# RMSNorm with swish on one core: all loads and stores on SyncE's queue in one order, with a ring of 100 rows

## The chip, the cores and the metric

The kernel runs on 1 core of one Trainium2 chip. The metric is the device time of one execution in microseconds (us). The kernel before takes 160.34 us, the median of 3 runs (160.22 to 160.51).

## The reference

The input `x` has 16 x 1024 rows of 512 float32 values; the output has the same shape. Each row is divided by its root mean square, multiplied by `gamma`, and then by its own sigmoid.

```
rms = sqrt(mean(x ** 2, axis=-1) + eps)
x_norm = x / rms * gamma
out = x_norm * (1 / (1 + exp(-x_norm)))        # float32
```

That is 16384 rows of 2 KB: 33.55 MB are read from HBM and 33.55 MB are written.

## The kernel before

The 16384 rows are spread over the 128 partitions, so that each partition holds 128 rows in the course of the run ("rows" below are always these 128 per partition; one such row is 256 KB over all partitions). The list `groups` (L28) says which rows are neighbours in HBM: within a group of n rows each partition's n rows are contiguous, so a transfer of a whole group moves one contiguous piece for each partition.

The rows live in a ring `xb` of 96 slots in SBUF (L29, L71). Row a uses slot a modulo 96, and everything is done in place: the load writes the slot, VectorE normalises it, ScalarE applies the swish, the store reads it. Rows 96 to 127 go into the slots of rows 0 to 31, so their loads have to wait for the stores of these rows.

The work is done in 32 chunks of 4 rows (`cn`, K = 32). For a chunk k:

- ScalarE squares it. Two of its rows are squared one by one with an accumulated sum (L181); the other two go to PSUM in one instruction (L188), and VectorE sums them (`sums`, L234).
- GpSimd adds eps and raises to the power -0.5 (L162, L169).
- VectorE multiplies each row by the scale and by gamma (`norm`, L245).
- ScalarE applies the swish to all four rows in one instruction (L200).

The order on ScalarE is written out by a loop (L223 to L230): the squares of chunk k, then those stores that are due, then the swish of chunk k - 2. VectorE does the sums of chunk k and then the norm of chunk k - 1. The first chunk that touches a newly loaded piece waits for that whole piece to land (L178).

Two queues carry the transfers. All ten loads (`load`, L118) are issued by SyncE in the order of the list `loads`; the first two stand ahead of the start barrier (`early`). Before a load that overwrites slots, SyncE waits until the stores of these slots have landed (L123); the table `behind` adds such a wait for load (96,16), which also waits for store (16,12). The eight stores (`store`, L206) are issued by ScalarE (L210) between its chunks. Each waits for the swish of its last chunk, and the table `hold` keeps the first three until load (64,28) has landed and store (64,32) until load (112,12) has landed. A piece (a, n) is the n rows from row a on. In the end SyncE waits for all stores (L267).

Of the kernel before, what the change touches and what calls it, by code (L numbers as in the profile page):

```python
# [9 lines left out]
def kernel(  # L10
# [7 lines left out]
    nc = tc.nc  # L18
# [5 lines left out]
    xf = x.flatten_outer_dims()  # L24
    of = out.flatten_outer_dims()
    R, D = xf.shape

    groups = [16, 16, 32, 32, 16, 16]  # L28
    ring = 96  # L29
    loads = [(0, 4), (4, 4), (8, 8), (16, 16), (32, 32), (64, 28)]  # L30
    loads += [(92, 4), (96, 16), (112, 12), (124, 4)]
    stores = [(0, 16), (16, 12), (28, 4), (32, 32), (64, 32)]
    stores += [(96, 16), (112, 8), (120, 8)]
    hold = {0: ((64, 28), 12), 3: ((112, 12), 22)}
    behind = {(96, 16): (16, 12)}
    early = 2
    cn = 4
    n_sq = 2
# [9 lines left out]
        assert sum(n for _, n in pieces) == rows_each  # L48

    K = rows_each // cn  # L50
    hold = {t: (loads.index(piece), k) for t, (piece, k) in hold.items()}
    behind = {loads.index(a): stores.index(b) for a, b in behind.items()}
    landings, seen = [], 0
    for k in range(K):
        landings.append([])
# [4 lines left out]
    ends = [-(-(a + n) // cn) for a, n in stores]  # L60
# [20 lines left out]
    ld = [nc.alloc_semaphore(f"ld{t}") for t in range(len(loads))]  # L81
    st = [nc.alloc_semaphore(f"st{t}") for t in range(len(stores))]
# [14 lines left out]
    s_swish = nc.alloc_semaphore("s_swish")  # L97

    def need(ins, sem, value):
        return ins.wait_op(sem, value, "sem-ge")  # L100

    def dram(ap, piece):
        a, n = piece
        g = max(g for g in range(len(groups)) if first[g] <= a)
        r = a - first[g]
        assert r + n <= groups[g], piece
        rows = ap[P * first[g] : P * (first[g] + groups[g])]
        return rows.rearrange("(p n) d -> p n d", n=groups[g])[:, r : r + n, :]

    def buf(piece):  # L110
        a, n = piece
        at = a % ring
        assert at + n <= ring, piece
        return xb[:, at : at + n, :]

    stored_by_sync = set()

    def load(i):  # L118
        a, n = loads[i]
        for u, (c, m) in enumerate(stores):  # L120
            over = c + ring < a + n and a < c + m + ring
            if (over or behind.get(i) == u) and u not in stored_by_sync:
                nc.sync.wait_ge(st[u], 16)  # L123
                stored_by_sync.add(u)
        return nc.sync.dma_start(  # L125
            out=buf(loads[i]), in_=dram(xf, loads[i])
        ).then_inc(ld[i], 16)

    entry = nc.main_func.blocks[0].instructions
    here = nc.cur_bb.bb.instructions  # L130
# [11 lines left out]
    for t in range(early):  # L142
        ins = load(t).ins
        assert here[-1] is ins or here[-1].name == ins.name
        here.pop()
        at = next(
            i for i, other in enumerate(entry)
            if other.engine == mybir.EngineType.SP
            and isinstance(other, mybir.InstDrain)
        )  # L150
        entry.insert(at, ins)
    for t in range(early, len(loads)):
        load(t)
    nc.sync.wait_ge(s_scratch, 16)

    nc.gpsimd.memset(blank, 0.0).then_inc(s_blank, 1)  # L156
# [3 lines left out]
    for k in range(K):  # L160
        need(
            nc.gpsimd.tensor_scalar(  # L162
                out=aeps[:, k, :], in0=ms[:, k, :], scalar1=eps_f, scalar2=None,
# [6 lines left out]
                out=rstd[:, k, :], in0=aeps[:, k, :], in1=neg_half, op=ALU.pow  # L170
# [4 lines left out]
    def square(k):  # L175
        at = k * cn % ring
        for landing in landings[k]:
            nc.scalar.wait_ge(ld[landing], 16)  # L178
        for j in range(n_sq, cn):
            n = k * (cn - n_sq) + j - n_sq  # L180
            acc = nc.scalar.activation(  # L181
                out=junk[n % 2], in_=xb[:, at + j, :], func=AF.Square,
                scale=inv_d**0.5, accum_out=ms[:, k, j : j + 1],
            )
            if n >= 2:
                need(acc, s_acc, n - 1)
            acc.then_inc(s_acc, 1)
        square = nc.scalar.activation(  # L188
            out=sq[k % 2], in_=xb[:, at : at + n_sq, :],
            func=AF.Square, scale=inv_d**0.5,  # L190
        )
        if k >= 2:
            need(square, s_sum, k - 1)
        square.then_inc(s_sq, 1)

    def swish(k):
        at = k * cn % ring
        rows = xb[:, at : at + cn, :]
        need(
            nc.scalar.activation(out=rows, in_=rows, func=AF.Silu), s_norm, k + 1  # L200
        ).then_inc(s_swish, 1)

    def after(t):
        return max((k for u, (_, k) in hold.items() if u <= t), default=0)

    def store(t):  # L206
        if t in hold:
            nc.scalar.wait_ge(ld[hold[t][0]], 16)
        need(
            nc.scalar.dma_start(out=dram(of, stores[t]), in_=buf(stores[t])),  # L210
            s_swish, ends[t],
        ).then_inc(st[t], 16)

    need(nc.scalar.dma_start(out=scratch, in_=blank), s_blank, 1).then_inc(
        s_scratch, 16
    )
# [2 lines left out]
        s_zero, 1,  # L219
    ).then_inc(s_gld, 16)  # L220
    nc.scalar.preload_act_table_set("silu_and_others")  # L221
    stored = 0
    for k in range(K + 3):  # L223
        if k < K:
            square(k)
        while stored < len(stores) and max(ends[stored] + 2, after(stored)) <= k:
            store(stored)
            stored += 1
        if 2 <= k < K + 2:
            swish(k - 2)  # L230

    def sums(k):
# [29 lines left out]
        if k >= 1:  # L262
            norm(k - 1)

    for t in range(len(stores)):
        if t not in stored_by_sync:
            nc.sync.wait_ge(st[t], 16)  # L267


# [33 lines left out]
```

## Time and profile before

| what | value |
|---|---|
| runs | 160.22, 160.34, 160.51 us |
| span of the profiled execution, first to last instruction | 159.3 us (159.28) |
| time of the profiled execution beside its span | not recorded apart; the median of the runs is 1.06 us above the span |
| ScalarE busy | 129.7 us |
| VectorE busy | 124.4 us |
| GpSimd busy | 65.4 us |
| bytes read and written, mean rate over the span | 33.56 MB and 33.56 MB, 421 GB/s |

The issues and landings of the transfers, from the trace (us from the start of the span; "landed" is when the last of the 16 DMA engines that share a transfer has reported):

| transfer | issued | landed |
|---|---|---|
| load (0,4) | 0.00 | 5.55 |
| load (8,8) | 1.90 | 13.04 |
| load (32,32) | 2.77 | 42.10 |
| load (64,28) | 3.27 | 59.04 |
| load (92,4) | 3.83 | 61.51 |
| store (0,16) | 59.11 | 72.06 |
| store (16,12) | 59.49 | 79.13 |
| store (28,4) | 60.60 | 81.53 |
| load (96,16) | 79.22 | 91.31 |
| load (112,12) | 79.58 | 98.58 |
| load (124,4) | 81.54 | 101.06 |
| store (32,32) | 98.66 | 120.41 |
| store (64,32) | 115.86 | 139.78 |
| store (120,8) | 146.47 | 159.23 |

How to read the profile: the page divides the span into 40 equal slices of about 4 us and gives each engine's busy share in tenths. The DMA row is the mean over the core's 16 DMA engines. A packet is counted with its whole duration and size in the slice where it starts, so slices with long packets swing around the mean. Each transfer is shared by the 16 DMA engines, 8 partitions each; each engine works through its own part, so that one transfer has 16 landings, one for each engine.

### The profile page before, as it was taken

To read this page: it belongs to the slowest core of one execution; us is meant where nothing else is said; L and a number is where in the kernel's file an instruction comes from. 1 tells how busy PE (TensorE), PEld (TensorE's weight loads), DVE (VectorE), ACT (ScalarE), POOL (GpSimd) and SP (SyncE) were. 2 spreads that over 40 slices of the span, in tenths; PEclk is the share of its full clock that TensorE was granted. 3 is DMA by queue.
4 is the path that set the end of the run, shared out by engine and by line. 5 is a ranking of instruction groups with operands and counts; after the bars stand their busy time and mean duration, and the time that the engine had idled before them with its cause. 6 is when DMAs were issued, how large, how long until landed. Compare 5 with 4: busy or idle time off the path is not lost.

```text
span 159.3 us, 503 instructions
## 1 busy us (share of the span) xinstructions
DVE 124.4 (78%) x162; ACT 129.7 (81%) x193; POOL 65.4 (41%) x71
## 2 busy tenths in 40 slices
DVE  0049996999289999599999999999999999992000
ACT  0675979997499995999999999999999999945000
POOL 1035553555145555155555555555555555540000
DMA  7999997998999969999899898969969969999997
GB/s 251 448 467 407 411 593 329 510 444 362 461 432 446 461 280 446 477 399 426 370 397 411 387 469 379 609 280 510 527 263 527 527 263 527 395 395 395 440 420 325
DMA packets 2750, 67.17 MB, mean 422 GB/s; under 512 B 437, under 2 KB 437, under 8 KB 441
## 3 DMA queue, kind: packets, MB, share of 16 engines
q1 hardware_dynamic: 1440, 33.56, 49.7%
q10 hardware_dynamic: 1304, 33.57, 49.0%
q14 instruction: 6, 0.04, 0.1%
HBM read 33.56 MB, written 33.56 MB: 421 GB/s over the span
## 4 chain that ended last, share of the span: by engine, by line
ACT 57%; DMA 25%; DVE 4%; issue 3%; ACTq 1%; SPq 0%
ACT xb L200 25%; DMA xb<-in_x_dram 25%; ACT junk L181 18%; ACT sq L188 14%; DVE xb L245 3%; ACTq L210 1%; DVE ms L234 1%; SPq L125 0%; ACTq L178 0%
## 5 line engine op out<-in xcount | busy, mean ns | idle before, releaser
L245 DVE SCALAR_TENSOR_TENSOR xb<-xb,rstd,gamma_sb 128x512 f32<-128x512 f32 x128 | 87.3, 744 | 0.0
L200 ACT ACTIVATE xb<-xb 128x2048 f32<-128x2048 f32 x32 | 60.9, 1903 | 5.0 <-DVE xb L245 3.4
L234 DVE TENSOR_REDUCE ms<-sq 128x2 f32<-128x1024 f32 x32 | 39.2, 1223 | 19.0 <-ACT sq L188 16.0
L162 POOL TENSOR_SCALAR aeps<-ms 128x4 f32<-128x4 f32 x32 | 20.6, 644 | 71.6 <-DVE ms L234 71.6
L169 POOL TENSOR_TENSOR rstd<-aeps,neg_half 128x4 f32<-128x4 f32 x32 | 44.0, 1376 | 2.7
L181 ACT ACTIVATE junk<-xb 128x512 f32<-128x512 f32 x64 | 37.2, 582 | 6.3 <-DMA xb<-in_x_dram 6.3
L188 ACT ACTIVATE sq<-xb 128x1024 f32<-128x1024 f32 x32 | 32.1, 1005 | 0.0
L181 ACT ACTIVATION_READ_ACCUMULATOR junk<-xb 128x1 f32 x64 | 11.9, 186 | 0.0
L221 ACT ACT_TABLE_LOAD x1 | 1.3, 1283 | 5.4 <-issue 5.4
L258 DVE LOAD_MASK_SELECT gamma_sb<-gamma x1 | 0.0, 14 | 1.1 <-DMA gamma<-in_gamma_dram 1.1
L258 DVE STREAM_SHUFFLE gamma_sb<-gamma 128x512 f32<-128x512 f32 x1 | 0.7, 716 | 0.0
L156 POOL MEMSET blank<- 128x16 f32 x1 | 0.1, 111 | 1.1 <-POOLq L66 1.1
L157 POOL MEMSET gamma<- 128x512 f32 x1 | 0.5, 524 | 0.0
L284 POOL MEMSET const-float32-0.0<- 128x1 f32 x1 | 0.1, 98 | 0.7 <-issue 0.7
L284 POOL MEMSET const-bfloat16-1.0<- 128x1 bf16 x1 | 0.1, 101 | 0.0
L284 POOL MEMSET const-uint8-127<- 128x1 uint8 x1 | 0.1, 101 | 0.0
L158 POOL MEMSET neg_half<- 128x4 f32 x1 | 0.1, 101 | 0.0
L284 POOL MEMSET const-float32-1.0<- 128x1 f32 x1 | 0.1, 99 | 0.0
## 6 DMA issues: line engine op xcount, KB each, us to landing
xb<-in_x_dram SPq DMA_DIRECT2D x2, 4096.0 KB, 16.3
out_dram<-xb ACTq DMA_DIRECT2D x2, 4096.0 KB, 15.3
xb<-in_x_dram SPq DMA_DIRECT2D x1, 7168.0 KB, 55.8
xb<-in_x_dram SPq DMA_DIRECT2D x4, 1024.0 KB, 13.6
out_dram<-xb ACTq DMA_DIRECT2D x2, 2048.0 KB, 13.7
out_dram<-xb ACTq DMA_DIRECT2D x1, 3072.0 KB, 19.6
xb<-in_x_dram SPq DMA_DIRECT2D x1, 3072.0 KB, 19.0
xb<-in_x_dram SPq DMA_DIRECT2D x1, 2048.0 KB, 11.1
```

What stands on the lines that cost most here:

```text
L157: nc.gpsimd.memset(gamma4, 0.0).then_inc(s_zero, 1)
L162: nc.gpsimd.tensor_scalar(out=aeps[:, k, :], in0=ms[:, k, :], scalar1=eps_f, scalar2=None, op0=ALU.add,),
L169: nc.gpsimd.tensor_tensor(out=rstd[:, k, :], in0=aeps[:, k, :], in1=neg_half, op=ALU.pow),
L181: acc = nc.scalar.activation(out=junk[n % 2], in_=xb[:, at + j, :], func=AF.Square, scale=inv_d**0.5, accum_out=ms[:, k, j : j + 1],)
L188: square = nc.scalar.activation(out=sq[k % 2], in_=xb[:, at : at + n_sq, :], func=AF.Square, scale=inv_d**0.5,)
L200: nc.scalar.activation(out=rows, in_=rows, func=AF.Silu), s_norm, k + 1
L210: nc.scalar.dma_start(out=dram(of, stores[t]), in_=buf(stores[t])),
L221: nc.scalar.preload_act_table_set("silu_and_others")
L234: nc.vector.tensor_reduce(out=ms[:, k, 0:n_sq], in_=sq[k % 2], op=ALU.add, axis=mybir.AxisListType.X,),
L245: ins = nc.vector.scalar_tensor_tensor(out=row, in0=row, scalar=rstd[:, k, j : j + 1], in1=gamma_sb, op0=ALU.mult, op1=ALU.mult,)
L258: nc.vector.stream_shuffle(gamma_sb, gamma4, [0] * 32), s_gld, 16
L284: nc = _bacc.Bacc("TRN2", target_bir_lowering=False, num_devices=1)
```

## The change

The transfers are cut and ordered anew, all of them on SyncE's queue. The ring has 100 slots instead of 96. The groups are 32, 48, 20 and 28 rows. There are 11 loads and 6 stores. A list `order` says what SyncE does: eight loads for rows 0 to 79; a wait until load (48,24) has landed; store (0,32); load (80,20), whose slots 80 to 99 are unused until then; a wait until store (0,32) has landed; loads (100,20) and (120,8) into the slots of rows 0 to 27; a wait until load (100,20) has landed; the stores of rows 32 to 127. Each store also waits for the swish of its last chunk, as before. ScalarE issues no stores any more, and its loop has nothing between the squares and the swish. The tables `hold` and `behind` go. The squares wait for the new, partly smaller pieces: rows 16 to 31 come in two loads of 8 rows where there was one of 16, and rows 32 to 79 in loads of 16, 24 and 8 rows. The sums, norms and swishes and their order stay as they are.

```diff
-    groups = [16, 16, 32, 32, 16, 16]
-    ring = 96
-    loads = [(0, 4), (4, 4), (8, 8), (16, 16), (32, 32), (64, 28)]
-    loads += [(92, 4), (96, 16), (112, 12), (124, 4)]
-    stores = [(0, 16), (16, 12), (28, 4), (32, 32), (64, 32)]
-    stores += [(96, 16), (112, 8), (120, 8)]
-    hold = {0: ((64, 28), 12), 3: ((112, 12), 22)}
-    behind = {(96, 16): (16, 12)}
+    groups = [32, 48, 20, 28]
+    ring = 100
+    loads = [(0, 4), (4, 4), (8, 8), (16, 8), (24, 8), (32, 16), (48, 24), (72, 8)]
+    loads += [(80, 20), (100, 20), (120, 8)]
+    stores = [(0, 32), (32, 32), (64, 16), (80, 20), (100, 20), (120, 8)]
+    order = [("load", a) for a in (0, 4, 8, 16, 24, 32, 48, 72)]
+    order += [("landed", 48), ("store", 0), ("load", 80)]
+    order += [("stored", 0), ("load", 100), ("load", 120)]
+    order += [("landed", 100)] + [("store", a) for a in (32, 64, 80, 100, 120)]
...
+    def store(t):
+        need(
+            nc.sync.dma_start(out=dram(of, stores[t]), in_=buf(stores[t])),
+            s_swish, ends[t],
+        ).then_inc(st[t], 16)
...
-    for t in range(early, len(loads)):
-        load(t)
+    for what, a in order[early:]:
+        if what == "load":
+            load(load_at[a])
+        elif what == "store":
+            store(store_at[a])
+        elif what == "landed":
+            nc.sync.wait_ge(ld[load_at[a]], 16)
+        else:
+            nc.sync.wait_ge(st[store_at[a]], 16)
     nc.sync.wait_ge(s_scratch, 16)
...
-    stored = 0
-    for k in range(K + 3):
+    for k in range(K + 2):
         if k < K:
             square(k)
-        while stored < len(stores) and max(ends[stored] + 2, after(stored)) <= k:
-            store(stored)
-            stored += 1
-        if 2 <= k < K + 2:
+        if k >= 2:
             swish(k - 2)
...
-    for t in range(len(stores)):
-        if t not in stored_by_sync:
+    waited = {a for what, a in order if what == "stored"}
+    for t, (a, _) in enumerate(stores):
+        if a not in waited:
             nc.sync.wait_ge(st[t], 16)
```

More of the change, by code (lines that the diff above doesn't have):

```diff
@@ L50 @@
     K = rows_each // cn
-    hold = {t: (loads.index(piece), k) for t, (piece, k) in hold.items()}
-    behind = {loads.index(a): stores.index(b) for a, b in behind.items()}
+    load_at = {a: t for t, (a, _) in enumerate(loads)}
+    store_at = {a: t for t, (a, _) in enumerate(stores)}
     landings, seen = [], 0
@@ L114, in buf, with load, check_order @@
         return xb[:, at : at + n, :]
[L116 to L127, printed above, removed]
+    def load(t):
+        return nc.sync.dma_start(
+            out=buf(loads[t]), in_=dram(xf, loads[t])
+        ).then_inc(ld[t], 16)
+    def store(t):
[3 more added lines that the diff above has]
+        ).then_inc(st[t], 16)
+    def check_order():
+        issued, stored = [], set()
+        for what, a in order:
+            if what == "stored":
+                stored.add(a)
+            if what == "load":
+                n = loads[load_at[a]][1]
+                for c, m in stores:
+                    if c + ring < a + n and a < c + m + ring:
+                        assert c in stored, (a, c)
+            issued.append((what, a))
+        assert [a for what, a in issued if what == "load"] == list(load_at)
+        assert [a for what, a in issued if what == "store"] == list(store_at)
+    check_order()
     entry = nc.main_func.blocks[0].instructions
@@ L151 @@
         entry.insert(at, ins)
-    for t in range(early, len(loads)):
-        load(t)
+    for what, a in order[early:]:
+        if what == "load":
+            load(load_at[a])
[5 more added lines that the diff above has]
+            nc.sync.wait_ge(st[store_at[a]], 16)
     nc.sync.wait_ge(s_scratch, 16)
@@ L201, in swish @@
         ).then_inc(s_swish, 1)
[L203 to L212, printed above, removed]
     need(nc.scalar.dma_start(out=scratch, in_=blank), s_blank, 1).then_inc(
```

## The prediction

> **What bounds the kernel now.** I read the slices of the page first, then the queues, then the waits of SyncE's queue, then windows around the one hole, and last the records of single DMA packets.
>
> ```profile
> span 159.3 us, 503 instructions
> DVE  0049996999289999599999999999999999992000
> ACT  0675979997499995999999999999999999945000
> DMA  7999997998999969999899898969969969999997
> GB/s 251 448 467 407 411 593 329 510 444 362 461 432 446 461 280 446 477 399 426 370 397 411 387 469 379 609 280 510 527 263 527 527 263 527 395 395 395 440 420 325
> q1 hardware_dynamic: 1440, 33.56, 49.7%
> q10 hardware_dynamic: 1304, 33.57, 49.0%
> HBM read 33.56 MB, written 33.56 MB: 421 GB/s over the span
> ```
>
> The two queues (q1 loads, q10 stores) together fill 98.7% of 16 DMA engines over the span. ScalarE and VectorE end three slices before the DMA does: the kernel is DMA-bound, and the page's chain, which ends on ScalarE at 146.4 us, names the wrong engine.
>
> ```profile
> SPq L123 <- DMA out_dram<-xb: 74.8, 1, 74.8
> SPq L125 <- DMA out_dram<-xb: 1.3, 1, 1.3
> 79.45:80.15 0.70, 0.70 (x2) 0.70 (x2) 0.62 (x2) 1.00 0.18 70
> 80.15:80.60 0.45, 0.45 (x2) 0.45 (x3) 0.45 (x1) 1.00 3.63 1001
> 80.60:81.15 0.55, 0.55 (x2) 0.55 (x3) 0.55 (x1) 1.00 0.54 209
> 81.15:81.95 0.80, 0.80 (x2) 0.80 (x2) 0.38 (x1) 1.00 0.00 0
> 81.95:82.55 0.60, 0.46 (x2) 0.60 (x2) 0.00 (x0) 1.00 2.06 874
> ```
>
> The windows (last two columns: DMA share and GB/s, each packet counted where it starts) show the only hole between start and end: SyncE's queue sits at L123 until store (16,12) has landed, and only then issues load (96,16). Packets start at 70 GB/s for 0.7 us, and after the burst at 80.15 nothing starts for 0.8 us. Spreading each packet's bytes over its duration, against a steady 434 GB/s, 1.22 us of transfer are missing from 79.5 to 82.5 us.
>
> Whether those 1.2 us set the end depends on the single engines. The packets chain exactly (each starts 4 ns before the last ends), so 16 chains can be followed. A 64 KB packet steps 2.414 us, a 32 KB one 1.209, an 8 KB one 0.305: 0.6025 us per row and engine, plus about 0.06 per DMA. Thirteen engines finish the first load phase at 59.84 to 60.22 us; three are late, C at 60.61, B at 60.91 and A at 61.07. The third queue tells why.
>
> ```profile
> q14 instruction: 3, 0.02, 8.6%
> ...
> q14 instruction: 1, 0.01, 1.9%
> ...
> q14 instruction: 1, 0.01, 1.9%
> ```
>
> These are the windows 2.6 to 3.3, 70 to 71 and 78 to 79 us: 8 KB instruction fetches on the same DMA engines. The three at 2.72, 2.92 and 3.12 us take 0.32 each, and the next 8 KB packets of those engines take 0.679, 0.941 and 0.884 instead of 0.309: costs of 0.69, 0.95 and 0.89 us. The one at 70.587 falls on B (0.309, and the next packet 1.372 instead of 0.912: 0.77), the one at 78.639 on A (0.309, next 0.502 instead of 0.309: 0.50). So the stores end at 79.55 to 79.85 on the thirteen, 80.02 on C, but 80.98 on A and 81.08 on B. In the hole the thirteen wait, and their first load packets take 1.69 to 2.2 us instead of 1.213. A and B go over with no gap, their first load packets (80.982 and 81.083) take 1.238 and 1.213, and at 82.22 and 82.30 they stand level with the others (82.00 to 82.49). The hole costs thirteen engines 1.2 to 1.5 us and the two latest ones nothing. At the end all data stop between 158.3 and 158.76, landings at 158.66 to 159.23.
>
> **The change part by part.** The sum is made for the profiled execution, span 159.28; the median of the runs is 160.34, so 1.06 us lie around the span, and I keep them.
>
> *The hole goes.* Load (80,20) goes to unused slots and stands in the ring behind store (0,32); loads (100,20) and (120,8) wait for store (0,32) while load (80,20), 20 x 0.6025 = 12.1 us, runs. For the thirteen this saves all of it. For A and B it saves nothing, and their lateness, which the hole absorbed, now lasts to the end.
>
> *The latest engines' new end.* The first 16 rows come by the same three loads; A has them at 12.58 us, B at 12.41, C at 12.12, the thirteen around 11.55. Then 240 rows x 0.6025 = 144.60 and 14 DMAs x 0.06 = 0.84: A 158.02, B 157.85, C 157.56, the thirteen 157.0. The mid-run fetches stay: ScalarE loses its store issues but gains waits for two more loads before that point, VectorE's program does not change, so each passes the same place a few us earlier. With what they cost before: A 158.52, B 158.62. Landing adds 0.46 (158.76 to 159.23), the last wait 0.03: **span 159.11, a gain of 0.17 us**. A fetch may cost from 0.31 (the fetch alone) to 0.95 (the dearest): A from 158.33 to 158.97, span 158.8 to 159.5.
>
> *Load-to-store handovers (at 50 and 99 us).* SyncE waits for load (48,24), then for load (100,20); behind each, 8 rows (4.8 us) are still queued. On A, load (48,24) lands near 47.0 (12.58 + 56 x 0.6025 + 0.24 + 0.45), the store's first packet comes 0.86 later (issue 59.11, packet 59.97), and the thirteen run out near 50.4: 2.5 us to spare. The second time 96.1 + 0.9 against 98.9: 1.9. A itself lost 0.04 at such a handover (61.07 to 70.75 for 16 rows), the thirteen 0.1 (second packets 1.27 instead of 1.213). I take 0.
>
> *The store-to-load handover (at 70 us), inside one ring.* Not in this trace. Below: 0, as A and B crossed over at 80.98 and 81.08, though from ring to ring. Above: 0.5 to 1.0, what the thirteen's first packets lost starting cold. I take 0: A and B cross when the others already read, as there. A gain is excluded, an engine cannot step faster than it does.
>
> The Trainium skill, "DMA: Bandwidth & Descriptors", section "Anatomy of one DMA", says that the semaphore fires only when the last byte is confirmed in the target memory and that this "can cause a surprisingly long delay especially when the write target is HBM". Read as a hold on the ring, it would cost the 0.46 us of a receipt here and give 160.6. By that rule stores in one ring would also stand apart; the trace disagrees, the next store's packets follow the semaphore write within 10 ns.
>
> *Issues moved.* Eight stores leave ScalarE's queue (0.34 to 1.40 us each, 4.5 in all), six go to SyncE's, which idles. Behind a waiting store on SyncE stand only later transfers that the same ring would serve later anyway. SyncE's one more load issue at the start may delay ScalarE's gamma issue (2.90 us) by about 0.5. All of this is hidden by the compute slack: ScalarE takes 4.0 us a chunk (the chain has squares at 103.78, 107.85, 111.86), and with loads in smaller pieces chunk 4 starts at 21.7 (22.83 before, after 1.07 idle), so swish 7 ends near 45.8, swish 24 near 114, swish 29 near 134 and swish 31 near 141. Needed: 47.0, 127, 139 and 151. Without that cover each us late would be a us on the end.
>
> *Piece sizes.* Seventeen DMAs for eighteen: 0.06 gained, in the sum above. Other row pitches: this trace holds whole and cut rows at the same rate; 0.
>
> Sum: 159.28 - 0.17 = 159.11; 160.34 - 0.17 = **160.2**.
>
> **The rivals.**
> - *The fetches miss:* mid-run fetches cost little, or fall on engines that are not late. A ends at 158.02, span 158.5, time 159.6. For it: their costs vary from 0.50 to 0.95 already; against: both fell on late engines.
> - *The rate rules, not the latest engine:* the missing 1.22 us are simply won: 159.1. For it: the windows; against: A's and B's unbroken chains.
> - *Slower, the store-to-load handover starts cold in one ring:* all 16 engines turn within 2 us, and first packets stretch on A and B as on the thirteen at 80.2. At 0.8 us the time is 161.0; it decides from 0.49 on (0.17 + 0.32). For it: no row shows the turn inside one ring; against: A's and B's 1.238 and 1.213.
> - *A handover comes too late:* SyncE single file leaves the ring dry at 50 or 99. The thirteen have 1.9 us to spare and 1.5 more behind A, and a cold start took 3.3 us from issue to full rate (79.22 to 82.5); a hole like that on A gives 161.3.
>
> **How the numbers follow.** Forecast 0.50 (own range 159.9 to 160.5), fetches miss 0.20, rate rules 0.08, cold turn 0.14, dry ring 0.08. A difference under 0.2% (0.32 us, 160.02 to 160.66) is about what a measurement of this kernel cannot tell from none. Faster: 0.20 + 0.08 + 0.11 of the forecast (its part under 160.02) = 0.39. Same: the forecast's other 0.39. Slower: 0.14 + 0.08 = 0.22. The range 159.3 to 161.0 leaves out the rate's case (0.08), the dry ring and the tail of the cold turn (0.11).
>
> **What the profile after would show.** Right: no slice from 2 to 38 with DMA below the others beyond packet counting; no SyncE wait that leaves the rings empty; 16 landings of the last store spread over 1.5 us instead of 0.57, the latest ones on engines with q14 packets; ScalarE done near 141. The forecast is wrong if the last landings lie within 0.6 us of each other (rate rules), if the fetches stand elsewhere or cost under 0.3, or if packets at 70 us take more than 0.1 us over their step on the latest engines.

## The result and the profile after

The changed kernel takes 161.07 us (median; 160.70 to 161.21) against 160.34 (160.02 to 160.51): a ratio of 1.0046, 95% interval 1.0035 to 1.0058. It is slower by 0.7 us; forecast were 160.2, with a range up to 161.0 and a chance of 0.22 for slower. The profiled execution has a span of 160.19 us (159.28 before).

The page of the changed kernel, its slices and queues:

```profile
span 160.2 us, 502 instructions
DVE  0049999999999999999999999999999999500000
ACT  0766999999999999999999999999999994800000
DMA  7999999999979979988998989999799999899893
GB/s 252 439 424 438 434 479 409 462 405 466 479 331 454 495 327 491 493 344 368 460 471 368 470 376 552 405 409 507 327 458 409 403 473 481 358 471 460 368 423 131
q1 hardware_dynamic: 2448, 67.11, 97.9%
```

One queue now carries everything. ScalarE is done at 140.2 us, 20 us before the end, without its earlier pauses; compute is not the limit: on the two engines that end last, the packets follow each other without a gap from load (72,8) to the end. The last slice is the first thing to see: 131 GB/s, where it was 325 before.

SyncE's waits, and four windows of the changed kernel (columns of a window: its length, busy time of VectorE, ScalarE and GpSimd, clock, DMA share, GB/s; each packet is counted whole in the window where it starts):

```profile
SPq L173 <- DMA xb<-in_x_dram: 65.5, 2, 42.1
SPq L118 <- DMA out_dram<-xb: 25.2, 1, 25.2
79.50:82.50 3.00, 2.90 (x5) 3.00 (x5) 1.31 (x2) 1.00 0.98 423
156.00:157.60 1.60, 0.00 (x0) 0.00 (x0) 0.00 (x0) 1.00 0.82 348
157.60:159.00 1.40, 0.00 (x0) 0.00 (x0) 0.00 (x0) 1.00 0.14 59
159.00:160.00 1.00, 0.00 (x0) 0.00 (x0) 0.00 (x0) 1.00 0.04 16
```

The hole at 80 us is gone (423 GB/s in the window where 1.2 us of transfer were missing). But the kernel ends on very few DMA engines: the last store lands on thirteen of them at 157.49 to 158.08 us, on the other three at 158.94, 159.43 and 160.14. That is the forecast picture. What was not forecast stands at the first change from loads to stores. The issue of load (48,24) and of load (72,8), KB and us from issue to landing:

```profile
xb<-in_x_dram SPq DMA_DIRECT2D x1, 6144.0 KB, 43.1
xb<-in_x_dram SPq DMA_DIRECT2D x1, 2048.0 KB, 48.5
```

Issued at 3.92 and 4.45, they land last at 47.03 and 53.00. The forecast had 47.0 and 51.9 (A's data at 51.44, which is 12.58 + 64 x 0.6025 + 5 x 0.06, and 0.45 to land). In the records of single packets the 16 KB packets of load (72,8) take 0.611 us as they should until 48.4. From 48.4 on 29 of them take over 0.7 us, up to 1.5, and 27 of these start before the first store packet does, at 50.64. On the two latest engines the piece takes 6.1 us instead of 4.9. Summed over all engines, the packets near 50 us run 0.63 us per engine over the usual duration for their size (the median of all packets of that size, 0.611 us for 16 KB). I call this sum the stretch below. It is a mean of 16 engines in one execution; an engine by itself can lose more.

### The profile page after: what moved, and what is told of

Read it like the earlier page. It is cut to its first block, busy times and chain, and to the rows that moved or that the text cites. A ratio compares the mean times of both kernels' runs of the same rounds, so it can differ in the third digit from the quotient of the medians.

```text
span 160.2 us, 502 instructions
## 1 busy us (share of the span) xinstructions
DVE 124.4 (78%) x162; ACT 129.4 (81%) x193; POOL 65.4 (41%) x71
## 4 chain that ended last, share of the span: by engine, by line
ACT 72%; DVE 6%; DMA 6%; issue 2%; POOL 0%; POOLq 0%
ACT xb L222 34%; ACT junk L203 22%; ACT sq L210 16%; DMA gamma<-in_gamma_dram 6%; DVE xb L252 5%; DVE ms L241 1%; DVE gamma_sb L265 0%; POOL gamma L179 0%; POOL blank L178 0%; POOLq L67 0%
```

## The experiments

Ratios are to the kernel before on the same chip. The kernels are called e1 to e12 below. The edits are shown shortened: the row numbers in `order` change with those in `loads` and `stores`.

**Is it the queued store, what follows it, or the piece itself?** e1, e2 and e3 change one of these each; e4 tests the other half of the forecast, that the latest engine sets the end.

```diff
# e1: the store waits for load (72,8)
-    order += [("landed", 48), ("store", 0), ("load", 80)]
+    order += [("landed", 72), ("store", 0), ("load", 80)]
# e2: only load (80,20) waits for load (72,8)
+    order += [("landed", 48), ("store", 0), ("landed", 72), ("load", 80)]
# e3: rows 72 to 79 in a group of their own, store (64,16) cut in two
-    groups = [32, 48, 20, 28]
+    groups = [32, 40, 8, 20, 28]
# e4: a hole for the early engines near 100 us
-    loads += [(80, 20), (100, 20), (120, 8)]
+    loads += [(80, 20), (100, 24), (124, 4)]
```

> Only the first wait is changed: store (0,32) is issued when load (72,8) has landed, not load (48,24). Theory 'queued store' (the store's or the following load's packets standing in the ring slow the load packets ahead of them): load (72,8) keeps its full rate and its last landing is at 51.9 us instead of 53.0; then the rings are dry until 52.9 and all engines start the store level, so the time is 161.4 to 162.0. Theory 'piece' (16 KB pieces at a 96 KB pitch read slowly late in the transfer, whatever stands behind): last landing still near 53.0 and a time of 162.5 to 163.2.

Measured: 162.79 us, ratio 1.0152 (1.0137 to 1.0168). Load (72,8), issued at 4.38, lands at 51.74, no packet stretched:

```profile
xb<-in_x_dram SPq DMA_DIRECT2D x1, 2048.0 KB, 47.4
```

So the store standing behind the loads does slow them. But the time is 0.8 us above what that theory gave: the stretch came back elsewhere, 0.90 us per engine at 70 us, at the change from stores to load (80,20), and 0.75 at 100 us. At 70 us it is above all the last store packets that are slow (64 KB in up to 3.54 us instead of 2.418), with load (80,20) queued behind them. This was the first hint that the place is not special.

> Store (0,32) is issued as in the changed kernel, load (80,20) only when load (72,8) has landed. If the load queued behind the store slows load (72,8): last landing of load (72,8) at 51.9 and a time near 160.0. If the queued store itself does it, or the piece: landing stays near 53.0, time 161.0 to 161.2.

Measured: 161.36 us, 1.0060 (1.0045 to 1.0075); load (72,8) lands at 53.28, stretch 0.84. The load behind the store is not the cause. (The time is 0.16 above its range.)

> Rows 72 to 79 get a group of their own in HBM (groups 32, 40, 8, 20, 28), so load (72,8) reads one contiguous stretch instead of 16 KB pieces 96 KB apart, and store (64,16) is cut in two. Theory 'piece': load (72,8) lands by 51.9, time near 160.0 to 160.2. Theory 'queued store': no change, landing near 53.0, time 161.0 to 161.3.

Measured: 161.37 us, 1.0066 (1.0049 to 1.0083); landing at 53.32, stretch 0.85. The way the piece lies in HBM is not the cause. (The time is 0.07 above its range.)

> The last two loads are cut 24 and 4 rows instead of 20 and 8, so store (32,32) is issued when only 4 rows are still to load: the rings of the thirteen early DMA engines run dry for 1.5 to 2 us near 100 us, those of the latest two do not. Theory 'the latest engine sets the end': the time stays at 160.9 to 161.3, and the 16 landings of the last store lie within 1.2 us instead of 2.65. Theory 'the transfer rate sets the end': the missing bytes come on top, 162.5 to 163.5.

Measured: 161.10 us, 1.0047 (1.0030 to 1.0064), the time of the changed kernel. The same windows of this kernel, first the hole, then the end:

```profile
94.00:99.00 5.00, 4.90 (x7) 5.00 (x11) 2.99 (x4) 1.00 0.82 352
99.00:103.00 4.00, 3.86 (x6) 4.00 (x8) 2.03 (x3) 1.00 0.84 354
...
156.00:157.60 1.60, 0.00 (x0) 0.00 (x0) 0.00 (x0) 1.00 1.15 492
157.60:159.00 1.40, 0.00 (x0) 0.00 (x0) 0.00 (x0) 1.00 0.88 374
159.00:160.00 1.00, 0.00 (x0) 0.00 (x0) 0.00 (x0) 1.00 0.09 33
```

And those of the changed kernel at the hole's place:

```profile
94.00:99.00 5.00, 4.90 (x8) 5.00 (x11) 3.07 (x3) 1.00 0.96 411
99.00:103.00 4.00, 3.86 (x6) 4.00 (x7) 2.04 (x3) 1.00 1.23 532
```

These windows count whole packets where they start, so their difference (1.0 MB) is too large for the hole. With each packet's bytes spread over its duration, 0.455 MB less is moved from 94 to 103 us, 1.05 us of transfer at 434 GB/s: fourteen engines start store (32,32) only at 100.85 to 101.00, after waits of about 0.6 to 1.7 us. The time does not change, where 1.05 us on top would give about 162.1. The last 16 landings now lie within 0.87 us (159.49 to 160.36) instead of 2.65. A hole that only the early engines see is free: this part of the forecast is shown.

Store (0,32) is issued behind load (48,24), with load (72,8) still queued, in e2, e3 and e4 too, and again in e7 and e9 below. They stretch 0.84, 0.85, 1.18, 0.90 and 0.97 at 50 us, so the 0.63 of the changed kernel is the least of six executions with this change, and differences of a few tenths between kernels mean little.

**Does it hang on how early the store is issued?** With a small last piece the store is issued when the early engines have little left to load.

```diff
# e5: a last piece of 4 rows
-    loads = [(0, 4), (4, 4), (8, 8), (16, 8), (24, 8), (32, 16), (48, 24), (72, 8)]
+    loads = [(0, 4), (4, 4), (8, 8), (16, 8), (24, 8), (32, 16), (48, 28), (76, 4)]
# e6: of 6 rows
+    loads = [(0, 4), (4, 4), (8, 8), (16, 8), (24, 8), (32, 16), (48, 26), (74, 6)]
# e7: the second change, queued earlier
-    loads += [(80, 20), (100, 20), (120, 8)]
+    loads += [(80, 20), (100, 12), (112, 16)]
# e8: the kernel before, two queues
-    loads = [(0, 4), (4, 4), (8, 8), (16, 16), (32, 32), (64, 28)]
-    loads += [(92, 4), (96, 16), (112, 12), (124, 4)]
+    loads = [(0, 4), (4, 4), (8, 8), (16, 16), (32, 32), (64, 24)]
+    loads += [(88, 8), (96, 16), (112, 12), (124, 4)]
...
-    hold = {0: ((64, 28), 12), 3: ((112, 12), 22)}
+    hold = {0: ((64, 24), 11), 3: ((112, 12), 22)}
```

> The changed kernel with loads (48,28) and (76,4) for (48,24) and (72,8): the wait stays on the load from row 48, so store (0,32) is issued when the early engines have 0.7 us of load left (3.5 before). Theory 'too early' (a store that enters the ring while load packets are still to be read slows them): no stretched load packets near 50 us, load (76,4) lands last at 52.0, time 160.0 to 160.4. Theory 'any first handover' (the loss comes with the change from loads to stores, whenever the store is issued): load (76,4) lands near 53, time 160.9 to 161.3.

Measured: 161.44 us, 1.0081 (1.0061 to 1.0102). Nothing is lost at 50 us (stretch 0.03, load (76,4) lands at 51.57), as "too early" said, but 0.74 is lost at 70 us and 0.81 at 99, where the changed kernel lost nothing. The forecast time was missed by 1 us.

> The same with loads (48,26) and (74,6): 1.9 us of load left on the early engines at the issue of store (0,32), about 1 us when its packets can stand in the ring. 'Too early': between the changed kernel and the one with 4 rows, 160.0 to 160.8, with few stretched packets. 'Any first handover': 160.9 to 161.3.

Measured: 161.25 us, 1.0065 (1.0050 to 1.0080). Stretch 0.11 at 50, 0.29 at 70, 0.19 at 99. Again out of the range of the theory that explained the place. The means hide where it falls: the two latest engines lose 0.62 and 0.65 us on load (74,6) (up to 4.34 us instead of 3.70), and the four latest lose 0.69 to 0.91 on load (120,8) (the last one 5.76 instead of 4.87), while the other twelve lose nothing there. On these engines over 3 us of load were left at the issue of the store at 50 us, and 2.9 us or more at 99, with 2.0 on the early ones.

> The changed kernel with loads (100,12) and (112,16) for (100,20) and (120,8): the second handover, at 99 us, which lost nothing, now has its store issued with 6.5 us of load left on the early engines (1.7 before). 'Too early': load packets before 99 us are stretched as they were before 50.6 us, and the time is 161.6 to 162.3. 'Any first handover': nothing is lost there, time 160.9 to 161.3.

Measured: 161.34 us, 1.0068 (1.0052 to 1.0084), stretch 0.05 at 99 although the store stood queued 7 us ahead. "Too early" alone has fallen. (The time is 0.04 above the range of the other theory.)

> The kernel before, two queues, with loads (64,24) and (88,8) for (64,28) and (92,4), and the first stores kept until load (64,24) has landed: they are issued at 56.7 us instead of 59.1, with 3.4 us of load left on the early engines. If stores that come too early slow loads whatever the queue, packets are stretched and the two latest engines lose 0.6 to 1.1 us: time 160.8 to 161.5. If it needs one ring: 160.2 to 160.6.

Measured: 161.39 us, 1.0076 (1.0059 to 1.0093). The two-queue kernel becomes as slow as the changed one when its first stores come 2.5 us earlier: load packets that start from 58.0 to 60.4 us are stretched, 0.88 us per engine, 30 of the 32 that take over 0.7 us before the first store packet starts at 60.28, and the latest engine ends its stores at 82.80 instead of 81.53. Window 58 to 62 of this kernel, and the same one of the kernel before:

```profile
58.00:62.00 4.00, 2.12 (x4) 4.00 (x7) 1.61 (x2) 1.00 1.09 377
```

```profile
58.00:62.00 4.00, 3.86 (x6) 2.40 (x6) 2.03 (x3) 1.00 1.08 457
```

So one ring is not needed for the loss. (Two rings also take turns here: load (88,8) ends at 65.07 on the latest engine, beside the stores.)

**The theory that was left: early and together.** In all these runs a direction change that is queued early loses 0.6 to 1.2 us per engine where the 16 engines come to it within about 1.3 us of each other, and little where they are over 2 us apart (0.01 to 0.05; in e6 0.19). The change from store (0,32) to load (80,20) at 70 us, queued 17 us ahead or more in each one-queue kernel up to here, goes the same way. Where the landings of the load piece before the store spread over 2.0 to 2.5 us it loses at most 0.03 (the changed kernel, e2, e3, e4, e7), over 1.7 us 0.29 (e6), over 1.1 us 0.74 (e5), and 0.90 in e1, where all engines started the store level. e9 to e12 test it.

```diff
# e9: the changed kernel, stores from row 32 on queued at 85 us
-    order += [("landed", 100)] + [("store", a) for a in (32, 64, 80, 100, 120)]
+    order += [("landed", 80)] + [("store", a) for a in (32, 64, 80, 100, 120)]
# e10: one queue, every change late
+    loads = [(0, 4), (4, 4), (8, 8), (16, 8), (24, 8), (32, 16), (48, 28), (76, 4)]
+    loads += [(80, 20), (100, 24), (124, 4)]
+    stores = [(0, 28), (28, 4), (32, 32), (64, 16), (80, 20), (100, 20), (120, 8)]
+    order += [("landed", 48), ("store", 0), ("store", 28)]
+    order += [("stored", 0), ("load", 80), ("load", 100), ("load", 124)]
# e11: e10 with ("landed", 80) for ("landed", 100)
# e12: e11 with loads (100, 20), (120, 8), as in e9
```

> The changed kernel, but SyncE waits for load (80,20) instead of load (100,20) before the stores of rows 32 and on, so store (32,32) stands in the ring from about 85 us, 14 us before the early engines change to it; packets of load (120,8) stay 16 KB. The engines arrive there 2.6 us apart. Theory 'early and together' (a direction change that is queued early loses time only if all 16 engines make it within about 1.3 us): nothing lost at 99 us, time 160.9 to 161.3. Theory 'early, with packets of 16 KB or less': load packets are stretched before 99 us, time 161.5 to 162.3.

Measured: 161.29 us, 1.0067 (1.0051 to 1.0082); stretch at 99 us 0.01.

> The changed kernel's one queue and its 80, 32, 48, 96 split, but every change of direction issued late behind a small piece: loads (48,28) and (76,4), stores (0,28) and (28,4), load (80,20) only when store (0,28) has landed, loads (100,24) and (124,4). If early queued transfers cause the loss: no stretched packets ahead of the three changes, the early engines wait for the late ones, and the time is 160.1 to 160.5, that of the kernel before. If one ring or the split itself costs: 160.8 to 161.4.

Measured: 160.58 us, 1.0025 (1.0016 to 1.0034). Nothing is stretched ahead of any change (0.06 at 50, 0.00 at 99); the 0.69 near 70 us are the early engines' first load packets after they had run dry, as before. It misses its range by 0.08 and is the best version with one queue, but still slower than the kernel before. In its trace the latest engine leaves the hole 0.47 us behind the next one (84.64 against 84.17) and ends 0.47 behind (159.62 against 159.15), where the kernel before comes out level; that this is the rest of the difference is argued, not shown.

> The kernel with three late changes, but the stores from row 32 on are issued when load (80,20) has landed, early again, with the engines close together there (less than 1 us apart) and 8 KB packets just ahead of the change. 'Early and together': load packets before 99 us are stretched, 0.5 to 0.8 us over the kernel with three late changes. 'Early, with 16 KB packets': no difference from it.

Measured: 162.41 us, 1.0138 (1.0123 to 1.0153): 1.8 us over the run with three late changes, where 0.5 to 0.8 were expected. The place and the sign are right (0.96 us stretched at 99), the size is not: on the latest engine load (124,4) took 4.15 us (99.33 to 103.48) instead of 2.5. Only the moment of issue differs between e10 and e11. Their windows from 99 to 103 us, e10 first:

```profile
99.00:103.00 4.00, 3.86 (x6) 4.00 (x7) 2.03 (x3) 1.00 1.39 600
```

```profile
99.00:103.00 4.00, 3.86 (x7) 4.00 (x7) 2.03 (x3) 1.00 1.10 391
```

Spread over the packets' durations this is 431 and 328 GB/s.

> The second change to stores is exactly that of the run with the wait on load (80,20): loads (100,20) and (120,8), store (32,32) queued 14 us early. Only the first 70 us differ: loads (48,28) and (76,4), stores (0,28) and (28,4), load (80,20) after store (0,28) has landed, so the engines come to the second change within 1.2 us of each other instead of 2.8. 'Early and together': 0.6 to 1.0 us of stretched load packets per engine before 99 us (0.01 there when they came apart), time 161.2 to 162.4. If the engines' distance does not matter: as little as in that run, time 160.5 to 160.8, that of three late changes.

Measured: 162.30 us, 1.0142 (1.0103 to 1.0180), stretch 0.96 at 99 us. (The profiled execution, 161.92, is the fastest of four that reach 163.41.) The windows of this run and then of the one with the same second change and the engines apart:

```profile
94.00:99.00 5.00, 4.90 (x8) 5.00 (x9) 3.05 (x3) 1.00 0.96 401
99.00:103.00 4.00, 3.86 (x6) 4.00 (x7) 2.05 (x2) 1.00 1.14 397
```

```profile
94.00:99.00 5.00, 4.90 (x7) 5.00 (x11) 2.99 (x4) 1.00 0.96 410
99.00:103.00 4.00, 3.86 (x6) 4.00 (x8) 2.03 (x3) 1.00 1.26 545
```

The pair differs only in the cutting and order of the first 80 rows' loads and the first 32 rows' stores, and so in how far apart the engines come to 99 us, and in when the three loads before it are issued (69.6 to 70.4 us here, 47.3 and 73.4 to 73.8 in e9); that this second difference does nothing is not shown by a run of its own. The last columns hold first store packets too. Spread over the packets' durations, 433 GB/s move from 99 to 103 us in e9 and 330 in e12. The changes from loads to stores side by side; "left" is what the early engines still have to load at the usual pace when the store is issued, "apart" the time from the first to the last landing of the piece before:

| kernel, change at | left, us | apart, us | stretch, us per engine |
|---|---|---|---|
| before, 60 | 0.8 | 1.2 | 0.06 |
| before, 100 | 1.7 | 0.4 | 0.00 |
| changed, 50 | 3.1 | 1.2 | 0.63 |
| changed, 99 | 1.8 | 2.7 | 0.01 |
| e1, 100 | 4.0 | 0.5 | 0.75 |
| e5, 50 | 0.9 | 1.2 | 0.03 |
| e5, 99 | 3.2 | 1.2 | 0.81 |
| e6, 50 | 2.0 | 1.2 | 0.11 |
| e6, 99 | 2.0 | 2.6 | 0.19 |
| e7, 99 | 7.0 | 2.4 | 0.05 |
| e8, 60 (two queues) | 3.2 | 1.2 | 0.88 |
| e9, 99 | 13.7 | 2.9 | 0.01 |
| e10, 100 | 1.1 | 1.1 | 0.00 |
| e11, 100 | 15.4 | 1.4 | 0.96 |
| e12, 99 | 15.7 | 1.0 | 0.96 |

## Why the prediction was wrong

**Right: the latest engine, not the rate, sets the end.** The hole's 1.2 us were won by the thirteen early engines and are worth nothing; that is visible in the last landings and shown by the run with an added hole (1.05 us of transfer, no change of time). The two rivals that hung on it, the whole 1.22 us won, or fetches that miss, did not come true.

**Wrong: "Load-to-store handovers: I take 0", at 50 us.** On the latest two engines load (72,8) cost 1.2 to 1.3 us more. The engine that came out last had its data of load (48,24) at 46.53 us, where I had B at 46.39 (+0.14), and took 6.09 us for load (72,8), where I had 4.88 (+1.21). It then took the fetch at 64.69, for 0.66 us instead of 0.77 (-0.11), 0.09 less for its other packets, and 0.37 to land instead of 0.46 (-0.09). Together this gives the last landing at 160.14 instead of 159.08. The handover is the one large term between the forecast span of 159.11 and the measured 160.19; the others nearly cancel, which is luck.

The step failed because I looked at such a change only for the store coming too late. My rows for it (59.11 and 98.66) had 0.8 and 1.7 us of load left at the issue; the change has 3.1, and I read the spare time as pure gain. The nearest rows were not near in the one respect that counted. The rivals on the slower side did not name it either. The cold turn had the place wrong: the turn from stores to loads at 70 us lost 0.02. The dry ring had a right place, 50 us, and the opposite fault, a store that comes too late; no ring ran dry, and that its 161.3 lies near the measured time is luck.

**The fetches** came at 64.69 and 68.55 us, a few us earlier, as forecast, but only one fell on a latest engine; the second hit the third latest (0.42). **Store to load inside one ring** costs nothing here (0.02), as taken; in e1 and e5 it cost 0.90 and 0.74, with the engines close together. **The semaphore receipt as a hold on the ring**, which I had weighed from the Trainium skill ("DMA: Bandwidth & Descriptors", "Anatomy of one DMA", a section on transfers that GpSimd issues), does not show: the slow packets belong to a load with the store still behind it, not to a transfer behind a finished one, and the 70 us change has no gap. **Moved issues, compute slack, piece sizes:** right, ScalarE ends at 140.2 (141 forecast), and no ring runs dry before its last store.

What stays open: why a queued change of direction slows the packets ahead of it, and why the distance of the three late engines matters when the thirteen early ones are within 0.7 us of each other in either case. The records show durations only. The runs show the two conditions, not a mechanism, and between 1.4 and 2.0 us apart there is one change alone (e6 at 70 us, 1.7 apart, 0.29). In e6 at 99 us (2.0 left, 2.6 apart, 0.19) only the four latest engines lost, 0.7 to 0.9 us each, though the three latest of the changed kernel, with 3.1 to 4.3 us left there, lost 0.03 at most.

## What to carry to other kernels

When transfers bound a kernel, follow each DMA engine by itself before pricing a hole: idle time that the latest engine does not share is worth nothing, and closing it also takes away the place where late engines catch up. A transfer in the other direction should be issued just ahead of need, here with 0.8 to 1.7 us of the old direction left on the early engines (a last piece of 4 rows, 1 MB; with 6 rows the two latest engines already lost 0.6 us), and not as early as possible (the kernel before did this at both its changes from loads to stores). Price a step from rows that agree with it in timing, not only in kind.

## What the runs showed of the hardware that was not expected

- A store queued behind 3 us or more of loads stretched the load packets ahead of it: 16 KB packets took up to 1.5 us instead of 0.611 in the changed kernel and up to 2.0 in e12, 0.6 to 1.2 us per engine in all, in one queue and in two. It did so hardly (0.01 and 0.05 us) where the engines came to the change 2.9 and 2.4 us apart.
- An avoided loss came back at the next change: without it at 50 us (0.03 instead of 0.63), 0.74 and 0.81 us appeared at 70 and 99 us in e5, where the engines were still 1.1 to 1.2 us apart.
- An 8 KB instruction fetch of 0.31 us delays the data of its DMA engine by 0.4 to 0.95 us, and the delay stays until the other engines run dry and this one does not.
